# Full-row score matmuls in both attention layers; in layer 1 the softmax statistics go between partitions by DMA, and ScalarE scales the probabilities

## The chip, the cores and the metric

The kernel runs on one core of a Trainium2 chip. The metric is the device time of one execution in microseconds: the median of several runs. The engines of a core work side by side, each through its own instructions in order: TensorE (PE in the profile; PEld is its weight load), VectorE (DVE), ScalarE (ACT), GpSimd (POOL) and SyncE (SP), which issues most DMAs.

## The reference

The reference is an encoder of two layers over 512 tokens of 1024 features with 16 heads of 64 features, all in float32. Each layer adds a token mixer and then a SwiGLU channel mixer to its input, each between two RMS norms:

```python
x = x + rms_norm(mixer(rms_norm(x, g1)), g2)
x = x + rms_norm(swiglu(rms_norm(x, g3), w_gate, w_up, w_down), g4)
```

Layer 0's mixer is neighbourhood attention: a grid of 8 rows by 64 columns, each query sees all 8 rows and 16 columns around it, with a learned bias. Layer 1's mixer is a mixture of three dilated windows, (window, dilation) = (128, 1), (512, 4) and (2048, 16). Each group has its own queries, keys and values, a distance penalty per head, and a softmax over its window; the three outputs are merged with weights proportional to the softmax denominators:

```python
outs.append(o); lses.append(lse)          # one attention output and one log-sum-exp per group
alpha = jax.nn.softmax(jnp.stack(lses, axis=0), axis=0)
o = jnp.einsum('gbsh,gbshd->bshd', alpha, jnp.stack(outs, axis=0))
```

## The kernel before

**Precision.** A float32 operand is split into a high part h (rounded by a ScalarE copy, L89) and a low part l (VectorE subtracts, L90). A projection takes three matmuls for one product: h x h, h x l, l x h (`mm3`, L101 to L103).

**Projections.** The products run as units of a seven-multiplication scheme (class `Seven`): a unit loads two weight blocks of 512 KB (`load2`, L85, into a ring of two buffers), adds pieces of them on GpSimd (L168 to L174), splits four operands (`h_a`, `l_a` to `h_c`, `l_c` and a small one), and runs 84 matmuls of 256 columns into one PSUM bank. `run` interleaves a unit's last steps with the next unit's first ones.

**Attention.** Heads go in pairs; eight pairs per layer. After a pair's queries and keys are there, `split_q` lays each head's queries into 128 partitions: the high part in the head's own 64 and the low part in the other 64. `split_k` does the keys: both halves of `k` hold the head's high part, and `kl` holds the low part in 64 rows only (L429, L430). A score block then takes two matmuls into one PSUM bank (`score3` and `window_softmax` in layer 0, L435, L436, L447, L448; `scores_a` in layer 1, L953, L954): one over 128 rows with the high part of the keys, and one over the head's 64 rows with the low part.

**Layer 1's loop.** A pair has three units, one per group. `scores_a` makes the local group's scores; `scores_b` the two dilated groups' (L967), from queries and keys in token order by residue, with plain float32 matmuls of 64 rows. A chunk of scores covers one head and two blocks of 128 queries. For each block, `softmax_pair` adds the bias and takes the minimum of the negated scores in one VectorE operation (L936), and ScalarE makes the exponentials with their sum (L937). GpSimd writes the biases from a table of distances into `bt` (L941). The probabilities lie in a ring of eight buffers, `p_`, of which one pair takes all eight; the score banks, tag `s`, are two.

The local group's rows are in another order than the dilated ones: partition 32r + n of block b against partition 32b + n of block r. To merge them, `weights` swaps the local statistics (16 columns: minimum and sum, two heads, four blocks) over 32-partition pieces by 16 VectorE copies (`swapped`, L911), forms the common minimum and the two factors by small VectorE operations and one exponential, and swaps the local factors back by 16 more copies. `finish` then scales the 16 probability blocks of the pair on GpSimd (L1009), transposes them on TensorE (L1023), copies them out of PSUM (L1024) and multiplies with the values (L1031, L1037). `keep` splits the output and stores it for the output projection (`yo`).

**Order.** Python code emits the program; a planner then orders each engine's instructions by a simulated time line with priorities in the order of emission. `between` hands up to four waiting score chunks to the next unit's run, and `done` calls `finish` when all chunks of a pair are through (`left`, eight at first). Each engine's queue, SP's too, is then executed in that order.

```python
cs, js = between()
run(unit_of(i), nxt, nxt, cs)
...
done(js)
if g == 0:
    add(scores_a, j)
if g == 2:
    add(scores_b, j)
```

Of the kernel before, what the change touches and what calls it, by code (L numbers as in the profile page):

```python
# [12 lines left out]
F32 = mybir.dt.float32  # L13
# [4 lines left out]
P = 128  # L18
# [20 lines left out]
def encoder_kernel(ctx: ExitStack, tc: tile.TileContext, a: dict, out: bass.AP):  # L39
# [383 lines left out]
    def split_k(k, kl, p):  # L423
        k = k.rearrange("p (h t) -> p h t", h=2)
        act.activation(k[0:64, 0], p[0:64], AF.Copy)
        act.activation(k[64:128, 1], p[64:128], AF.Copy)
        dve.tensor_copy(k[64:128, 0], p[0:64])
        dve.tensor_copy(k[0:64, 1], p[64:128])
        dve.tensor_sub(kl[0:64], p[0:64], k[0:64, 0].bitcast(F32))  # L429
        dve.tensor_sub(kl[64:128], p[64:128], k[64:128, 1].bitcast(F32))  # L430
        return k, kl

    def score3(o, q, kd, kl, hd, qs, ks, start=True):
        r = slice(64 * hd, 64 * hd + 64)
        i = pe.matmul(o, q[(ALL, hd) + qs], kd[(ALL, hd) + ks], start=start, stop=False, skip_group_check=True)  # L435
        pe.matmul(o, q[(r, hd) + qs], kl[(r,) + ks], start=False, stop=True, skip_group_check=True)  # L436
        return i
# [4 lines left out]
    def window_softmax(q, kd, kl, hd, bt, pr, mn, sm, name):  # L442

        sb = [bank("s", f"s{name}_{i}") for i in range(2)]
        kw = kd[:, hd].rearrange("p (b t) -> p b t", b=4)[:, 0:4:3, :]
        kwl = kl[64 * hd:64 * hd + 64].rearrange("p (b t) -> p b t", b=4)[:, 0:4:3, :]
        i0 = pe.matmul(sb[0][:, 0:256], q[:, hd, 0:P], kw, start=True, stop=False, skip_group_check=True)  # L447
        pe.matmul(sb[0][:, 0:256], q[64 * hd:64 * hd + 64, hd, 0:P], kwl, start=False, stop=True,  # L448
                  skip_group_check=True)
# [374 lines left out]
    q_, k_, kl_ = ring(rxc, 0, 1152, 2), ring(rxc, 2304, D, 2), ring(rxc, 4352, 512, 2)  # L824
# [50 lines left out]
    q_, k_, kl_, ost_ = rxc[:, 0:D], rxc[:, D:2 * D], ring(rxc, 2 * D, 512, 2), ring(rxc, 3 * D, D, 1)  # L875
    w22_ = w22_ring(rxc[:, 4 * D:5 * D])
    b6 = bt.rearrange("p (k c) -> p k c", c=P)
    nc.gpsimd.dma_start(dist, a["dist"])
# [28 lines left out]
    def swapped(out_, in_):  # L907

        for i in range(4):
            for k in range(4):  # L910
                dve.tensor_copy(out_[32 * k:32 * k + 32, :, i], in_[32 * i:32 * i + 32, :, k])  # L911

    def weights(sa, sb, few):


        ta, d, w, mn, ga = (few[:, i:i + n] for i, n in ((32, 16), (48, 16), (64, 16), (80, 8), (88, 8)))
        swapped(ta.rearrange("p (s k) -> p s k", k=4), sa.rearrange("p (s k) -> p s k", k=4))
        dve.tensor_tensor(mn, ta[:, 0:8], sb[:, 0:8], op=ALU.min)
        dve.tensor_sub(d[:, 0:8], mn, ta[:, 0:8])
        dve.tensor_sub(d[:, 8:16], mn, sb[:, 0:8])  # L920
        act.activation(d, d, AF.Exp)
        dve.tensor_mul(w[:, 0:8], d[:, 0:8], ta[:, 8:16])
        dve.tensor_mul(w[:, 8:16], d[:, 8:16], sb[:, 8:16])
# [3 lines left out]
        dve.tensor_mul(w[:, 8:16], d[:, 8:16], mn)  # L927
        swapped(ga.rearrange("p (s k) -> p s k", k=4), w[:, 0:8].rearrange("p (s k) -> p s k", k=4))
        return ga, w[:, 8:16]

    def softmax_pair(pr, s, bts, st, c):

        for i in range(2):
            f = slice(256 * i, 256 * i + 256)
            o, v = (m[:, f].rearrange("p (k c) -> p k c", k=2) for m in (pr, s))
            dve.tensor_tensor_reduce(o, v, bts[i], -1.0, BIG, ALU.add, ALU.min, st[:, c + i:c + i + 1])  # L936
            act.activation(pr[:, f], pr[:, f], AF.Exp, bias=st[:, c + i:c + i + 1], scale=-1.0,  # L937
                           accum_out=st[:, 8 + c + i:9 + c + i])

    def bias(j, hd, c):  # L940
        pool.tensor_scalar(bt[:, c], dist[:, c], SLOPES[2 * j + hd], 1.0, op0=ALU.mult, op1=ALU.mult)  # L941

    def scores_a(j, hd, b2):
        rw = slice(64 * hd, 64 * hd + 64)
# [3 lines left out]
        for b in (2 * b2, 2 * b2 + 1):  # L948

            k2, l2 = ((v.rearrange("p (i t) -> p i t", i=4)[:, 0:4:3] if b == 0 else  # L950
                       v[:, P * b - P:P * b + P]) for v in (kd[:, hd], kl[rw]))
            dst = s[:, b % 2 * 256:b % 2 * 256 + 256]
            i = pe.matmul(dst, q[:, hd, block(b)], k2, start=b % 2 == 0, stop=False, skip_group_check=True)  # L953
            pe.matmul(dst, q[rw, hd, block(b)], l2, start=False, stop=True, skip_group_check=True)  # L954
            i0 = i if b % 2 == 0 else after(i, i0)
        softmax_pair(pr, s, ((b6[:, 1:3], b6[:, 0:2]), (b6[:, 0:2], b6[:, 0:4:3]))[b2], stats[j][0], 4 * hd + 2 * b2)
        parts[0, j, hd, b2] = pr

    def scores_b(j, hd, c2):
        rw = slice(64 * hd, 64 * hd + 64)  # L960
        if c2 == 0:
            bias(j, hd, slice(4 * P, 6 * P))
        s, pr = bank("s", f"sb_{j}_{hd}_{c2}"), next(p_)
        for c in (2 * c2, 2 * c2 + 1):
            for g in range(2):
                f0, (qf, kf) = c % 2 * 256 + g * P, qk[3 * j + 1 + g]
                pe.matmul(s[:, f0:f0 + P], qf[rw, block(c)], kf[rw, block(c)], start=True, stop=True)  # L967
        softmax_pair(pr, s, (b6[:, 4:6], b6[:, 4:6]), stats[j][1], 4 * hd + 2 * c2)
        parts[1, j, hd, c2] = pr

    def chunks(f, j):
        return [partial(f, j, hd, c) for hd in range(2) for c in range(2)]
# [29 lines left out]
    def finish(j):  # L1002
        ga, gb = weights(*stats[j])
        pts = []
        for hd in range(2):
            for a_b, w in enumerate((ga, gb)):
                for b in range(4):
                    v = parts[a_b, j, hd, b // 2][:, b % 2 * 256:b % 2 * 256 + 256]
                    pool.tensor_scalar(v, v, w[:, 4 * hd + b:4 * hd + b + 1], 1.0, op0=ALU.mult, op1=ALU.mult)  # L1009
# [61 lines left out]
    for n, i in enumerate(order):  # L1071
        j, g = divmod(i, 3)
        if n % 3 == 0:
            few, left[j] = next(few_), 8
            stats[j] = few[:, 0:16], few[:, 16:32], few
# [3 lines left out]
        if g == 0:  # L1079
            q = q_.rearrange("p (h t) -> p h t", h=2)  # L1080
            split_q(q, qs)
            kd, kl = split_k(k_, next(kl_), ks)
# [108 lines left out]
```

## Time and profile before

| | us |
|---|---|
| median of 3 runs (lowest, highest) | 1648.68 (1645.87, 1654.98) |
| profiled execution | 1645.9 |
| its span | 1644.1 |
| TensorE busy | 1536.3 (93%) |
| VectorE busy | 1263.6 (77%) |
| ScalarE busy | 850.2 (52%) |
| GpSimd busy | 685.7 (42%) |
| layer 0's attention loop, about | 65 to 250 |
| layer 1's attention loop, about | 830 to 1246 |

In the profile's rows, `L954` is line 954 of the kernel, the names are out<-in tiles without their numbers, and `128*128 128x256` is a matmul's rows * columns of weights and the partitions x elements of the moving operand. In the timeline a row has start, duration, engine and operation, and in brackets the idle time before it and what ended it. Matmuls overlap, and their ends are modelled: the distance from one start to the next says what one costs.

### The profile page before, as it was taken

The numbers are of one execution on the slowest core, as the hardware profiler recorded it, in microseconds if no ns is written. First come the engines' busy times: TensorE is split into PE (matmuls) and PEld (weight loads), VectorE is DVE, ScalarE is ACT, GpSimd is POOL, SyncE is SP. The second block draws the span as 40 slices with busy tenths as digits, with TensorE's granted clock in tenths as the row PEclk, the third lists the DMA queues.
The fourth block names the chain that finished last, engine by engine and source line by source line (L and its number), as shares of the span: only waits on it lengthen the run. The fifth ranks groups of instructions, "written<-read, shape, count | busy, mean of one in ns | idle before, by whom it ended". The sixth has DMA issues, their size and how long they took to land.

```text
span 1644.1 us, 28158 instructions
## 1 busy us (share of the span) xinstructions
PE 1536.3 (93%) x10788; PEld 1387.7 (84%) x10788; DVE 1263.6 (77%) x2140; ACT 850.2 (52%) x1659; POOL 685.7 (42%) x622
## 2 busy tenths in 40 slices
PE   7999999799999898879999999999998799999896
PEld 7977767799999686879988887888876799999684
DVE  5478864889998877677688788697865699998866
ACT  5356653455555555434465456455553455555554
POOL 3345432733330122465556655565613633330221
PEclk9999999899999999999999999999999899999999
DMA  4322353322322996545321231221545233323994
GB/s 167 118 66 97 122 202 128 141 78 106 120 83 71 251 239 177 175 133 163 116 84 53 78 116 65 104 77 65 195 140 169 88 103 104 103 78 97 251 243 115
DMA packets 66248, 208.80 MB, mean 127 GB/s; under 512 B 7040, under 2 KB 17280, under 8 KB 66112
## 3 DMA queue, kind: packets, MB, share of 16 engines
q1 hardware_dynamic: 53936, 164.91, 29.4%
q0 software_dynamic: 12032, 41.82, 10.6%
q8 instruction: 85, 1.39, 0.4%
q14 instruction: 51, 0.42, 0.1%
q10 hardware_dynamic: 144, 0.26, 0.0%
HBM read 184.94 MB, written 22.02 MB: 126 GB/s over the span
## 4 chain that ended last, share of the span: by engine, by line
PE 65%; DVE 14%; DMA 9%; issue 6%; POOL 3%; ACT 3%; SPq 0%; POOLq 0%; DVEq 0%; ACTq 0%
PE gu L101 9%; PE gu L102 9%; PE gu L103 9%; PE pp_d L101 3%; PE pp_d L103 3%; PE pp_d L102 3%; DMA raw<-wd 3%; DVE ap L911 2%; DMA wd<-wd 2%; PE t L1023 2%; PE yo L101 1%; PE sb L967 1%; PE yo L103 1%; PE yo L102 1%; PE pp_n L101 1%
## 5 line engine op out<-in xcount | busy, mean ns | idle before, releaser
L103 PE MATMUL gu<-rxc,l_a 128*128 128x256 f32 x352 | 102.2, 291 | 2.9 <-DVE l_a L90 2.9
L101 PE MATMUL gu<-rxc,h_a 128*128 128x256 f32 x352 | 102.8, 294 | 0.0
L102 PE MATMUL gu<-rxc,h_a 128*128 128x256 f32 x352 | 102.7, 292 | 0.0
L101 PE MATMUL gu<-rxa,h_c 128*128 128x256 f32 x352 | 100.2, 285 | 0.7 <-DVE fg L558 0.4
L101 PE MATMUL gu<-rxa,h_b 128*128 128x256 f32 x352 | 99.7, 284 | 0.2 <-ACT rxa L324 0.2
L102 PE MATMUL gu<-rxa,h_b 128*128 128x256 f32 x352 | 99.8, 284 | 0.0
L103 PE MATMUL gu<-rxa,l_c 128*128 128x256 f32 x352 | 99.6, 283 | 0.0
L102 PE MATMUL gu<-rxa,h_c 128*128 128x256 f32 x352 | 99.6, 283 | 0.0
L103 PE MATMUL gu<-rxa,l_b 128*128 128x256 f32 x352 | 99.5, 283 | 0.0
L937 ACT ACTIVATE ap<-ap 128x256 f32<-128x256 f32 x128 | 64.0, 502 | 57.0 <-DVE ap L936 56.3
L600 POOL DMA_DIRECT2D wd<-wd x36 | 34.3, 999 | 140.8 <-DVE l_d1p L90 50.3
L168 POOL TENSOR_TENSOR fg<-fg 128x512 f32<-128x512 f32 x24 | 39.8, 1657 | 121.0 <-DVE l_a L90 119.8
L168 POOL TENSOR_TENSOR r_gu<-r_gu 128x512 f32<-128x512 f32 x20 | 35.5, 1773 | 116.3 <-DVE l_a L90 116.3
L168 POOL TENSOR_TENSOR r_d<-r_d 128x512 f32<-128x512 f32 x24 | 38.0, 1584 | 97.7 <-DVE l_ad L90 97.7
L89 ACT ACTIVATE rxc<-hid 128x512 fp32r<-128x512 f32 (+1 forms) x84 | 49.2, 590 | 53.2 <-PE yd_s L102 32.8
L1009 POOL TENSOR_SCALAR ap<-ap 128x256 f32<-128x256 f32 x128 | 69.2, 560 | 15.4 <-DVE ap L927 15.2
L103 PEld LDWEIGHTS gu<-rxc,l_a 128*128 128x128 f32 x352 | 70.2, 199 | 3.1 <-DVE l_a L90 3.1
L101 PEld LDWEIGHTS gu<-rxc,h_a 128*128 128x128 f32 x352 | 70.3, 200 | 0.5 <-ACT rxc L324 0.5
L102 PEld LDWEIGHTS gu<-rxc,h_a 128*128 128x128 f32 x352 | 70.4, 200 | 0.0
L101 PEld LDWEIGHTS gu<-rxa,h_c 128*128 128x128 f32 x352 | 67.5, 192 | 1.7 <-DVE fg L558 1.5
L101 PEld LDWEIGHTS gu<-rxa,h_b 128*128 128x128 f32 x352 | 67.6, 193 | 0.5 <-ACT rxa L324 0.5
L102 PEld LDWEIGHTS gu<-rxa,h_c 128*128 128x128 f32 x352 | 67.5, 192 | 0.2
(590 smaller groups left out, 6366.7 us busy)
## 6 DMA issues: line engine op xcount, KB each, us to landing
r_d<-dil_qk SPq DMA_DIRECT2D x48, 512.0 KB, 4.5
r_d<-wd SPq DMA_DIRECT2D x30, 512.0 KB, 4.5
wd<-wd POOLq DMA_DIRECT2D x30, 512.0 KB, 9.6
fg<-wg SPq DMA_DIRECT2D x24, 512.0 KB, 3.7
fg<-wu SPq DMA_DIRECT2D x24, 512.0 KB, 4.6
r_gu<-wg SPq DMA_DIRECT2D x20, 512.0 KB, 3.7
r_gu<-wu SPq DMA_DIRECT2D x20, 512.0 KB, 4.6
r_n<-na_qk SPq DMA_DIRECT2D x16, 512.0 KB, 4.4
```

The source lines that it names most:

```text
L89: act.activation(h, src, AF.Copy)
L101: i = pe.matmul(o, s[0], m[0], start=start, stop=False, skip_group_check=True)
L102: pe.matmul(o, s[0], m[1], start=False, stop=False, skip_group_check=True)
L103: pe.matmul(o, s[1], m[0], start=False, stop=stop, skip_group_check=True)
L168: e[0].tensor_add(q[0], q[0], q[2])
L600: nc.gpsimd.dma_start(v, src, accum_op=ALU.add)
L911: dve.tensor_copy(out_[32 * k:32 * k + 32, :, i], in_[32 * i:32 * i + 32, :, k])
L937: act.activation(pr[:, f], pr[:, f], AF.Exp, bias=st[:, c + i:c + i + 1], scale=-1.0, accum_out=st[:, 8 + c + i:9 + c + i])
L967: pe.matmul(s[:, f0:f0 + P], qf[rw, block(c)], kf[rw, block(c)], start=True, stop=True)
L1009: pool.tensor_scalar(v, v, w[:, 4 * hd + b:4 * hd + b + 1], 1.0, op0=ALU.mult, op1=ALU.mult)
L1023: pe.transpose(t[:, block(i)], part(a_b, *blocks[4 * n + i]), ident)
```

## The change

Scores: `kl` becomes as wide as `k`, one half of the columns per head, with zeros in the 64 rows that are not the head's own. The matmul with the low part then runs over all 128 rows. Layer 0 has two such buffers (one of them a new tile), zeroed once; layer 1 has one, zeroed before the first pair.

Strided scores of layer 1: a chunk now makes both heads' scores for two query blocks, the matmuls of the two heads alternating, into two banks; a pair has two such chunks in place of four, so `left` starts at 6. Both heads' biases are written first, the second head's where the local bias lies.

Statistics: the two swaps of `weights` are now one DMA to a small DRAM tile and four DMAs back each, on SP's queue; the columns are in another order (block, then minimum and sum, then head), so that each piece of a row is contiguous. `finish` scales the probabilities by ScalarE activations.

```diff
     def split_k(k, kl, p):
...
-        dve.tensor_sub(kl[0:64], p[0:64], k[0:64, 0].bitcast(F32))
-        dve.tensor_sub(kl[64:128], p[64:128], k[64:128, 1].bitcast(F32))
+        kl = kl.rearrange("p (h t) -> p h t", h=2)
+        dve.tensor_sub(kl[0:64, 0], p[0:64], k[0:64, 0].bitcast(F32))
+        dve.tensor_sub(kl[64:128, 1], p[64:128], k[64:128, 1].bitcast(F32))
+    def zero_rows(kl):
+        pool.memset(kl[64:128, :512].bitcast(F32), 0.0)
+        pool.memset(kl[0:64, 512:].bitcast(F32), 0.0)
+        return kl
     def score3(o, q, kd, kl, hd, qs, ks, start=True):
-        r = slice(64 * hd, 64 * hd + 64)
         i = pe.matmul(o, q[(ALL, hd) + qs], kd[(ALL, hd) + ks], start=start, stop=False, skip_group_check=True)
-        pe.matmul(o, q[(r, hd) + qs], kl[(r,) + ks], start=False, stop=True, skip_group_check=True)
+        pe.matmul(o, q[(ALL, hd) + qs], kl[(ALL, hd) + ks], start=False, stop=True, skip_group_check=True)
...
-    def swapped(out_, in_):
-        for i in range(4):
-            for k in range(4):
-                dve.tensor_copy(out_[32 * k:32 * k + 32, :, i], in_[32 * i:32 * i + 32, :, k])
+    sw = [dpool.tile([P, 16], F32, name=f"sw{i}") for i in range(4)]
+    def swapped(out_, in_, d, n):
+        nc.sync.dma_start(d[:, :4 * n], in_)
+        for k in range(4):
+            nc.sync.dma_start(out_[32 * k:32 * k + 32].rearrange("p (i s) -> p i s", s=n),
+                              d[:, n * k:n * k + n].rearrange("(i p) s -> p i s", i=4))
...
-        swapped(ta.rearrange("p (s k) -> p s k", k=4), sa.rearrange("p (s k) -> p s k", k=4))
+        swapped(ta, sa, sw[j % 2], 4)
...
-        swapped(ga.rearrange("p (s k) -> p s k", k=4), w[:, 0:8].rearrange("p (s k) -> p s k", k=4))
+        swapped(ga, w[:, 0:8], sw[2 + j % 2], 2)
...
     def scores_a(j, hd, b2):
...
-            pe.matmul(dst, q[rw, hd, block(b)], l2, start=False, stop=True, skip_group_check=True)
+            pe.matmul(dst, q[:, hd, block(b)], l2, start=False, stop=True, skip_group_check=True)
...
-    def scores_b(j, hd, c2):
+    def scores_b(j, c2):
         if c2 == 0:
-            bias(j, hd, slice(4 * P, 6 * P))
-        s, pr = bank("s", f"sb_{j}_{hd}_{c2}"), next(p_)
+            bias(j, 0, slice(4 * P, 6 * P))
+            bias(j, 1, slice(4 * P, 6 * P), bt[:, 0:2 * P])
+        ss = [bank("s", f"sb_{j}_{hd}_{c2}") for hd in range(2)]
         for c in (2 * c2, 2 * c2 + 1):
             for g in range(2):
                 f0, (qf, kf) = c % 2 * 256 + g * P, qk[3 * j + 1 + g]
-                pe.matmul(s[:, f0:f0 + P], qf[rw, block(c)], kf[rw, block(c)], start=True, stop=True)
+                for hd in range(2):
+                    rw = slice(64 * hd, 64 * hd + 64)
+                    pe.matmul(ss[hd][:, f0:f0 + P], qf[rw, block(c)], kf[rw, block(c)], start=True, stop=True)
...
     def finish(j):
...
-                    pool.tensor_scalar(v, v, w[:, 4 * hd + b:4 * hd + b + 1], 1.0, op0=ALU.mult, op1=ALU.mult)
+                    act.activation(v, v, AF.Copy, scale=w[:, 2 * b + hd:2 * b + hd + 1])
...
-            few, left[j] = next(few_), 8
+            few, left[j] = next(few_), 6
```

More of the change, by code (lines that the diff above doesn't have):

```diff
@@ L444, in window_softmax @@
         sb = [bank("s", f"s{name}_{i}") for i in range(2)]
-        kw = kd[:, hd].rearrange("p (b t) -> p b t", b=4)[:, 0:4:3, :]
-        kwl = kl[64 * hd:64 * hd + 64].rearrange("p (b t) -> p b t", b=4)[:, 0:4:3, :]
+        kw, kwl = (v[:, hd].rearrange("p (b t) -> p b t", b=4)[:, 0:4:3, :] for v in (kd, kl))
         i0 = pe.matmul(sb[0][:, 0:256], q[:, hd, 0:P], kw, start=True, stop=False, skip_group_check=True)
-        pe.matmul(sb[0][:, 0:256], q[64 * hd:64 * hd + 64, hd, 0:P], kwl, start=False, stop=True,
-                  skip_group_check=True)
+        pe.matmul(sb[0][:, 0:256], q[:, hd, 0:P], kwl, start=False, stop=True, skip_group_check=True)
         src = [sb[0][:, 256:512], sb[1][:, 0:256], sb[1][:, 256:512]]
@@ L823, in encoder_kernel @@
     qs_, ks_, p5_ = ring(ap, 7296, 512, 2), ring(ap, 8320, 512, 2), ring(ap, 9344, 256, 2)
-    q_, k_, kl_ = ring(rxc, 0, 1152, 2), ring(rxc, 2304, D, 2), ring(rxc, 4352, 512, 2)
+    akl = inner.enter_context(arena("akl", D, "right", F32R))
+    q_, k_, kl_ = ring(rxc, 0, 1152, 2), ring(rxc, 2304, D, 2), cycle([zero_rows(v) for v in (akl, rxc[:, 4352:])])
     vq = [v_quarter(apv[:, qd * D:(qd + 1) * D], a["na_v"][qd], f"n{qd}",
@@ L874, in encoder_kernel @@
     qs, ks, p5_ = ap[:, c0 + 1728:c0 + 2240], ap[:, c0 + 2240:c0 + 2752], ring(ap, c0 + 2752, 256, 2)
-    q_, k_, kl_, ost_ = rxc[:, 0:D], rxc[:, D:2 * D], ring(rxc, 2 * D, 512, 2), ring(rxc, 3 * D, D, 1)
+    q_, k_, kl_, ost_ = rxc[:, 0:D], rxc[:, D:2 * D], rxc[:, 2 * D:3 * D], ring(rxc, 3 * D, D, 1)
     w22_ = w22_ring(rxc[:, 4 * D:5 * D])
     b6 = bt.rearrange("p (k c) -> p k c", c=P)
+    b2h = b6[:, 4:6], b6[:, 0:2]
     nc.gpsimd.dma_start(dist, a["dist"])
@@ L927, in weights, with softmax_pair @@
         dve.tensor_mul(w[:, 8:16], d[:, 8:16], mn)
-        swapped(ga.rearrange("p (s k) -> p s k", k=4), w[:, 0:8].rearrange("p (s k) -> p s k", k=4))
+        swapped(ga, w[:, 0:8], sw[2 + j % 2], 2)
         return ga, w[:, 8:16]
-    def softmax_pair(pr, s, bts, st, c):
+    def softmax_pair(pr, s, bts, st, hd, b2):
         for i in range(2):
@@ L935, in softmax_pair, with bias @@
             o, v = (m[:, f].rearrange("p (k c) -> p k c", k=2) for m in (pr, s))
[L936 to L941, printed above, removed]
+            c = 4 * (2 * b2 + i) + hd
+            dve.tensor_tensor_reduce(o, v, bts[i], -1.0, BIG, ALU.add, ALU.min, st[:, c:c + 1])
+            act.activation(pr[:, f], pr[:, f], AF.Exp, bias=st[:, c:c + 1], scale=-1.0, accum_out=st[:, c + 2:c + 3])
+    def bias(j, hd, c, o=None):
+        o = bt[:, c] if o is None else o
+        pool.tensor_scalar(o, dist[:, c], SLOPES[2 * j + hd], 1.0, op0=ALU.mult, op1=ALU.mult)
     def scores_a(j, hd, b2):
-        rw = slice(64 * hd, 64 * hd + 64)
         if b2 == 0:
@@ L966, in scores_b @@
                 f0, (qf, kf) = c % 2 * 256 + g * P, qk[3 * j + 1 + g]
-                pe.matmul(s[:, f0:f0 + P], qf[rw, block(c)], kf[rw, block(c)], start=True, stop=True)
-        softmax_pair(pr, s, (b6[:, 4:6], b6[:, 4:6]), stats[j][1], 4 * hd + 2 * c2)
-        parts[1, j, hd, c2] = pr
+                for hd in range(2):
+                    rw = slice(64 * hd, 64 * hd + 64)
+                    pe.matmul(ss[hd][:, f0:f0 + P], qf[rw, block(c)], kf[rw, block(c)], start=True, stop=True)
+        for hd in range(2):
+            pr = next(p_)
+            softmax_pair(pr, ss[hd], (b2h[hd], b2h[hd]), stats[j][1], hd, c2)
+            parts[1, j, hd, c2] = pr
     def chunks(f, j):
+        if f is scores_b:
+            return [partial(f, j, c) for c in range(2)]
         return [partial(f, j, hd, c) for hd in range(2) for c in range(2)]
@@ L1002, in finish @@
     def finish(j):
-        ga, gb = weights(*stats[j])
+        ga, gb = weights(*stats[j], j)
         pts = []
@@ L1081, in encoder_kernel @@
             split_q(q, qs)
-            kd, kl = split_k(k_, next(kl_), ks)
+            if j == 0:
+                zero_rows(kl_)
+            kd, kl = split_k(k_, kl_, ks)
         done(js)
```

21 lines of the change are left out of this document (12 added, 9 removed).

## The prediction, made before the result was known

> **What bounds the kernel now.** I read the stage table first: it gives each engine's busy time in a stretch, then the granted clock and the DMA share. The first row is layer 0's attention loop, the second layer 1's.
>
> ```profile
> 65.00:222.00 157.00, 150.41 (x973) 123.37 (x973) 121.86 (x274) 95.42 (x219) 76.59 (x95) 0.98 0.32 108
> 845.00:1250.00 405.00, 390.04 (x2919) 342.39 (x2918) 314.21 (x825) 210.39 (x535) 214.94 (x252) 0.99 0.29 98
> ```
>
> TensorE is idle for 157.00 - 150.41 = 6.6 us of the first and 405.00 - 390.04 = 15.0 us of the second; VectorE is busy 78% in both, ScalarE 61% and 52%, GpSimd 49% and 53%. TensorE is what both loops wait for. But busy is not productive, so I read the timeline of TensorE next, by the distance from one start to the next. Layer 1's local scores (L953 has 128 rows, L954 64), then layer 0's:
>
> ```profile
> 1214.70 0.28 PE L953 MATMUL sa<-rxc 128*128 128x256 f32 x1
> 1214.91 0.38 PE L954 MATMUL sa<-rxc 64*128 64x256 f32 x1
> 1215.22 0.38 PE L953 MATMUL sa<-rxc 128*128 128x256 f32 x1
> 1215.53 0.38 PE L954 MATMUL sa<-rxc 64*128 64x256 f32 x1
> 1215.84 0.50 PE L103 MATMUL yo<-rxb,rxa 128*128 128x512 f32 x1
> ```
>
> ```profile
> 162.78 0.38 PE L436 MATMUL s<-rxc 64*128 64x256 f32 x1
> 163.09 0.39 PE L435 MATMUL s<-rxc 128*128 128x256 f32 x1
> ```
>
> and a projection, where all have 128 rows, up to the longest stall of layer 1's loop:
>
> ```profile
> 1023.29 0.28 PE L102 MATMUL pp_d<-rxb,rxc 128*128 128x256 f32 x1
> 1023.41 0.28 PE L103 MATMUL pp_d<-rxb,rxc 128*128 128x256 f32 x1
> 1029.22 0.58 PE L103 MATMUL pp_d<-rxa,l_ad 128*128 128x256 f32 x1 [5.53 <-DVE l_ad L90]
> ```
>
> With equal rows a 256-column matmul starts 0.12 us after the one before. Where 128 and 64 rows alternate, the four take 0.21, 0.31, 0.31 and 0.31 us, 0.285 in the mean. The stall at 1023.41 is the other thing to see. VectorE's timeline says what l_ad waited behind:
>
> ```profile
> 1021.56 6.35 DVE L911 COPY ap<-ap 32x2 f32<-32x2 f32 x16
> 1027.94 1.23 DVE L90 TENSOR_TENSOR l_ad<-r_d,h_ad 128x1024 fp32r<-128x1024 f32 x1
> ```
>
> Sixteen statistics copies held the split that TensorE needed next.
>
> **Part 1, full-row scores.** No matmul is added or removed: the low-part ones get 128 rows, half of them zeros. The counts, from the groups of layer 1 and the view of layer 0's tile s:
>
> ```profile
> L954 PE MATMUL sa<-rxc 64*128 64x256 f32 x64 | 24.4, 381 | 0.0
> L953 PE MATMUL sa<-rxc 128*128 128x256 f32 x64 | 22.6, 353 | 0.0
> ```
>
> ```profile
> L435 PE MATMUL s<-rxc x48: 279/385/388, 99.9 to 248.3; 128*128 128x256 f32 x48
> L436 PE MATMUL s<-rxc x48: 378/382/382, 100.2 to 248.7; 64*128 64x256 f32 x48
> L447 PE MATMUL s<-rxc x16: 276/279/385, 99.3 to 246.6; 128*128 128x256 f32 x16
> L448 PE MATMUL s<-rxc x16: 379/381/383, 99.5 to 246.8; 64*128 64x256 f32 x16
> ```
>
> 128 matmuls in each layer, each from 0.285 to 0.12 us: 128 x 0.165 = 21.1 us of TensorE per layer. The Trainium skill speaks against it: TensorEngine Tiling (Array Packing), Theoretical Speedup, gives up to 2x for packing contractions of 64 rows or fewer, so by that page filling them up with zeros gives a saving away. The rows have a half-row matmul at 0.31 us and a full one at 0.12, and the measurement decides.
>
> In layer 0 nothing else changes but four half memsets on GpSimd at the start. What TensorE gives up is not all gained: its time falls to 150.41 - 21.1 = 129.3 us while VectorE keeps 121.86 us of work, in a chain with it (score, reduction, exponential, transposition). Bounds: -21 (all arrives) to -5 (157 falls to 152, VectorE's queue decides). I take two thirds, **-14 us**, since TensorE remains the longer.
>
> **Part 2, the strided scores, both heads alternating (L967).** Same count, 256. Today sixteen take 952.13 - 950.15 = 1.98 us:
>
> ```profile
> 950.15 2.05 PE L967 MATMUL sb<-ap 64*128 64x128 f32 x16
> 952.13 0.39 PE L102 MATMUL pp_d<-rxa,h_ad 128*128 128x256 f32 x1
> ```
>
> which is 0.124 each. Alternating row halves cost at least half of that if two run side by side (-0.062 x 256 = -15.9 us), and the same if they don't. I take a quarter, -4 us, nearer to the row, since all 64-row matmuls of the trace run one after another. The Trainium skill is more hopeful: TensorEngine Tiling (Array Packing), Key Properties, says that different tiles can load and multiply in parallel; by it the -15.9 us would be an estimate of the whole. No run so far shows it.
>
> **Part 3, copies to DMAs, scaling to ScalarE.**
>
> ```profile
> L1009 POOL TENSOR_SCALAR ap<-ap 128x256 f32<-128x256 f32 x128 | 69.2, 560 | 15.4 <-DVE ap L927 15.2
> L937 ACT ACTIVATE ap<-ap 128x256 f32<-128x256 f32 x128 | 64.0, 502 | 57.0 <-DVE ap L936 56.3
> L911 DVE COPY ap<-ap 32x4 f32<-32x4 f32 (+1 forms) x256 | 54.8, 214 | 4.5 <-ACT ap L937 0.6
> ```
>
> VectorE loses 54.8 us (6.9 per pair of heads), GpSimd 69.2. ScalarE gets 128 scalings; none is in the trace, the nearest row is the exponential of the same form, 502 ns: 64 us, 8.0 per pair, so it goes from 210 to about 275 busy, still under TensorE. They come sixteen in a row ahead of ScalarE's weight splits, where the copies stood ahead of VectorE's; cover taken for cover given.
>
> Two moves cost nothing. The low part of the keys has one buffer in layer 1 instead of two, but the queries and the high part have one already, so the same matmuls are waited for. And the second head's strided bias is written where the local bias lies, so the next local bias waits for its reductions; GpSimd waits for these today, with little behind it:
>
> ```profile
> POOL ap L941 <- DVE ap L936: 51.9, 17, 17.0
> ```
>
> Without that cover it would be one bias, 0.7 us per pair.
>
> The exchange is one store and four loads, twice per pair, 80 DMAs, issued by SP. Landing times and an issue:
>
> ```profile
> vd<-ap SPq DMA_DIRECT2D x20, 256.0 KB, 2.1
> ...
> ep<-spill SPq DMA_DIRECT2D x8, 64.0 KB, 6.5
> ```
>
> ```profile
> 1246.01 0.42 SPq L1103 DMA_DIRECT2D ep<-spill  x1
> ```
>
> One exchange: issue 0.42, store 2.1, four issues 1.7, last load 2.1, together 6.3 us when the queue is free, or 0.42 + 6.5 + 1.7 + 6.5 = 15.1 when crowded. With 3.5 us for the small sums on VectorE between the two exchanges and about 2 for the first four scalings, the way from the last exponential to the first transposition is X = 12.6 + 5.5 = 18 us, at most 36. I take 18: the second stage row has DMA busy at 0.29 only. Today's X and the period of a pair of heads, from the last exponentials of pairs 1, 2 and 7 and pair 2's first transposition:
>
> ```profile
> 913.79 0.50 ACT L937 ACTIVATE ap<-ap 128x256 f32<-128x256 f32 x1
> ...
> 967.34 0.49 ACT L937 ACTIVATE ap<-ap 128x256 f32<-128x256 f32 x1
> ...
> 1225.54 0.49 ACT L937 ACTIVATE ap<-ap 128x256 f32<-128x256 f32 x1
> ```
>
> ```profile
> 982.70 0.27 PE L1023 MATMUL t<-ident,ap 128*128 128x128 f32 x1
> ```
>
> The period is (1226.03 - 914.29) / 6 = 52.0 us and X = 982.70 - 967.83 = 14.9, so 37.1 us lie elsewhere in the cycle (transpositions, values, the next strided and local scores). The cycle closes because the eight probability buffers are all one pair's: the next pair's scores wait for this pair's transpositions, and in the new order the first chunk wants a second head's buffer, which is freed last.
>
> If TensorE alone sets the period, it is 52.0, less its idle 15.0 / 8 = 1.9, less (21.1 + 4) / 8 = 3.1: 47.0 us. If the cycle is strict, it is 37.1 - 3.1 + 18 = 52.0: nothing gained. Much of the 37.1 is waiting behind projection matmuls, so neither holds; I take 50.0. Over seven periods that is **-14 us**, bounds -35 to 0. It holds part 2 and the removed stalls.
>
> SP waits in order, up to 21 us for a weight buffer:
>
> ```profile
> SPq L85 <- DVE l_cd L90: 143.5, 10, 21.0
> ```
>
> A load behind an exchange is late by its wait for the statistics; these long waits are the cover, as a load has most of a unit to arrive. An exchange behind such a wait would be the worse case, the third rival.
>
> The last pair has no next pair to hide behind. Its first transposition:
>
> ```profile
> 1236.16 1.03 PE L1023 MATMUL t<-ident,ap 128*128 128x128 f32 x8
> ```
>
> 10.1 us after 1226.03, filled with output-projection matmuls to the end. With X = 18 TensorE lacks work for 8 us, less what the planner saves up for it: **+6 us** (0 to 16). The memsets of layer 1 add at most **+1**.
>
> **Sum.** -14 - 14 + 6 + 1 = -21 us. The profiled execution took 1645.9 us (span 1644.1); it becomes 1624.9. The median of the runs lies 2.8 us higher, 1648.7, so I predict 1628 for the changed kernel's median.
>
> **Rivals.** *The whole saving arrives.* For it: TensorE idles only 4% in either loop. Against: VectorE has 121.86 us to do in layer 0. Layer 1 -35, layer 0 -20, tail +5: -50, 1599 us.
>
> *ScalarE becomes the late engine.* Sixteen scalings, 8.0 us, stand ahead of the splits of the next unit, as the sixteen copies did at 1021.56. For it: that stall was 5.5 us behind 6.35. Against: it happened once in eight pairs. If half of it recurs in each, 8 x 2.8 = 22 us eat the 21: about 1649, no change.
>
> *The exchange sets the period: slower.* Place: SP's queue, where a store waits for its landing before four loads go, and 512 KB weight loads lie in between. With two of the four landings at 4.1 instead of 2.1 X is 22, the strict cycle 56.0 us, so 7 x 4.0 = +28, layer 0 -14, tail +10, memsets +1: +25, 1674 us. It makes the kernel slower as soon as the cycle is strict and 8X - 151 exceeds 8, that is above X = 20. For it: the 6.5 us row, and the longest SP waits. Against: 37.1 has slack, as TensorE was never idle in it. The Trainium skill speaks for this rival: DMA: Bandwidth & Descriptors, Rules for kernel authors, wants small transfers joined and calls those under 64 KB mostly overhead.
>
> **Chances.** Forecast 0.45, whole saving 0.25, ScalarE late 0.15, exchange 0.15. Half a per cent, 8 us, is about what a measurement of this kernel tells from none. Faster is 0.45 + 0.25 = 0.70, same 0.15, slower 0.15. The range runs from 1594 (just under the whole saving) to 1664, most of the way to the slow case; the forecast's own is 1610 to 1645.
>
> **What would show it.** Full rows: starts 0.12 us apart in both score groups, no 64-row form left there. Layer 0's loop: about 143 us instead of 157. The exchange: X near 18, and SP landings near 2.1 for the small DMAs. The cycle: last exponentials 50 us apart, 47 if TensorE alone sets it, 52 or more if strict. ScalarE: a wait of TensorE for an h or l split right behind sixteen scalings. The tail: a TensorE gap of some 6 us before the last transpositions and a lower granted clock behind it. I am wrong if small DMAs land at 4 us or more in the loop, or if layer 0 doesn't get faster while its starts are 0.12 apart.

## The result and the profile after

The changed kernel takes **1608.05 us** (median of 4 runs, 1605.10 to 1608.84), the kernel before 1648.72. The ratio is 0.9745, with a 95% interval of 0.9715 to 0.9775: about 41 us faster. In a second measurement it was 0.9741 (0.9719 to 0.9762); below I use 0.9743 for it, and turn ratios into times with 1649 us. Forecast were 1628 us and a gain of 21. So the direction was right, and the gain was about twice the forecast.

Where the 41 us come from is read from a few marks in each trace. The view by tile gives for each group the first and the last start. The first fence is the kernel before (transpositions of the output stage, local scores, transpositions of probabilities), the second the changed kernel:

```profile
L322 PE MATMUL tr_o<-ident,ep x112: 270/273/478, 283.6 to 1306.6; 128*128 128x128 f32 x112
L953 PE MATMUL sa<-rxc x64: 276/385/388, 832.1 to 1223.8; 128*128 128x256 f32 x64
L1023 PE MATMUL t<-ident,ap x256: 270/272/421, 882.2 to 1242.5; 128*128 128x128 f32 x128
```

```profile
L322 PE MATMUL tr_o<-ident,ep x112: 270/273/476, 264.3 to 1266.9; 128*128 128x128 f32 x112
L969 PE MATMUL sa<-rxc x64: 277/283/387, 813.5 to 1178.8; 128*128 128x256 f32 x64
L1046 PE MATMUL t<-ident,ap x256: 270/273/476, 855.7 to 1204.0; 128*128 128x128 f32 x128
```

| mark | before | after | gain so far |
|---|---|---|---|
| layer 0's attention done (first tr_o) | 283.6 | 264.3 | 19.3 |
| layer 1's loop begins (first sa) | 832.1 | 813.5 | 18.6 |
| last local scores (last sa) | 1223.8 | 1178.8 | 45.0 |
| last transposition (last t) | 1242.5 | 1204.0 | 38.5 |
| end of the span | 1644.1 | 1603.3 | 40.8 |

Layer 0 gives 19 us, layer 1's loop 26, and the way from the last scores to the last transposition takes 6.5 back. I call the stretch from the first sa to the last t layer 1's loop: 410.4 us before, 390.5 after.

**Full rows.** The timeline of TensorE shows local scores of the changed kernel at the same distance as a projection:

```profile
1030.59 0.28 PE L969 MATMUL sa<-rxc 128*128 128x256 f32 x1
1030.71 0.28 PE L970 MATMUL sa<-rxc 128*128 128x256 f32 x1
1030.83 0.28 PE L969 MATMUL sa<-rxc 128*128 128x256 f32 x1
```

From start to start the 128 of them take 16.7 us in all, before 38.0. The 128 of layer 0 take 19.1 us, before 37.3, so 18 less.

**Alternating heads.** Sixteen strided scores, from their start to the next matmul's:

```profile
922.27 1.49 PE L986 MATMUL sb<-ap 64*128 64x128 f32 x16
923.69 0.38 PE L101 MATMUL pp_d<-rxb,rxc 128*128 128x256 f32 x1
```

That is 1.42 us, where it was 1.98. In 73 of the 220 steps inside such groups the next matmul, of the other head, starts within 10 ns, and the pair together takes the 0.11 us that one took alone. The steps inside groups add up to 20.7 us instead of 28.2; with the steps out of them the strided scores fall from 37.4 to 29.5.

**The exchange.** Its DMAs by group (KB of each, median us from issue to landing), then an exchange in SP's timeline:

```profile
ap<-sw SPq DMA_DIRECT2D x32, 2.0 KB, 1.7
ap<-sw SPq DMA_DIRECT2D x32, 1.0 KB, 1.7
sw<-ap SPq DMA_DIRECT2D x8, 8.0 KB, 1.4
sw<-ap SPq DMA_DIRECT2D x8, 4.0 KB, 1.4
```

```profile
983.96 0.33 SPq L919 DMA_DIRECT2D sw<-ap  x1
985.37 1.75 SPq L921 DMA_DIRECT2D ap<-sw  x4
```

From the store's issue to the last load's landing this one took 4.5 us (983.96 to 988.5), which is also the median of the 16. Two exchanges, at 1084.45 and 1133.81, took 7.1 and 9.3 us, as their loads landed only after 4.3 to 6.1 us. Now the last exponentials of pairs 1 and 7, and the last pair's first transposition:

```profile
885.12 0.50 ACT L954 ACTIVATE ap<-ap 128x256 f32<-128x256 f32 x1
...
1180.84 0.49 ACT L954 ACTIVATE ap<-ap 128x256 f32<-128x256 f32 x1
```

```profile
1194.31 2.10 PE L1046 MATMUL t<-ident,ap 128*128 128x128 f32 x8 [2.67 <-ACT ap L1032]
```

The period is (1181.33 - 885.62) / 6 = 49.3 us, before 52.0. X, the way from a pair's last exponential to its first transposition, is 12.2, 12.6, 17.9, 19.5, 17.9, 20.2, 17.3 and 13.0 us for the eight pairs. The last of them ends in an idle TensorE, and in the table by stage the granted clock (third from the end, ahead of DMA share and GB/s) of the tail is lower than in the loop:

```profile
813.00:1190.00 377.00, 358.65 (x2890) 327.65 (x2889) 264.12 (x601) 258.20 (x665) 156.81 (x127) 0.99 0.33 106
1190.00:1204.00 14.00, 10.48 (x50) 6.88 (x48) 2.07 (x3) 8.06 (x19) 0.00 (x0) 0.76 0.03 1
```

Last, what TensorE waits for in layer 1's loop (total us, times, longest). Before, then after; rows under 1 us are left out:

```profile
PE pp_d L103 <- DVE l_ad L90: 5.5, 1, 5.5
PE pp_d L101 <- DVE ap L406: 5.3, 6, 1.5
PE pp_d L101 <- DVE pp_d L158: 1.2, 1, 1.2
PE pp_d L101 <- DVE ap L409: 1.2, 1, 1.2
```

```profile
PE sb L986 <- ACT ap L412: 5.5, 3, 3.0
PE pp_d L101 <- DVE ap L406: 5.2, 3, 3.3
PE t L1046 <- ACT ap L1032: 2.7, 1, 2.7
PE yo L101 <- ACT h_wo L89: 2.0, 1, 2.0
PE t L1046 <- ACT ap L1047: 1.9, 1, 1.9
PE pp_d L101 <- ACT h_ad L89: 1.2, 3, 0.4
PE pp_d L101 <- DVE ap L409: 1.1, 2, 0.7
```

The stall behind the copies (l_ad) is gone, and ScalarE's rows are new.

### The profile page after: what moved, and what is told of

Same layout as the page of the kernel before. It is cut to its first block, busy times and chain, and to the rows that moved or that the text cites. A ratio compares the mean times of both kernels' runs of the same rounds, so it can differ in the third digit from the quotient of the medians.

```text
span 1603.3 us, 28068 instructions
## 1 busy us (share of the span) xinstructions
PE 1486.7 (93%) x10788; PEld 1366.7 (85%) x10788; DVE 1205.0 (75%) x1884; ACT 897.6 (56%) x1787; POOL 628.1 (39%) x500
## 4 chain that ended last, share of the span: by engine, by line
PE 61%; DVE 12%; DMA 11%; issue 6%; ACT 5%; POOL 4%; SPq 1%; POOLq 0%; DVEq 0%; ACTq 0%
PE gu L101 9%; PE gu L102 9%; PE gu L103 9%; PE pp_d L101 4%; PE pp_d L102 3%; PE pp_d L103 3%; DMA raw<-wd 3%; DMA wd<-wd 2%; PE t L1046 2%; PE sb L986 1%; ACT ap L1032 1%; PE vd L102 1%; PE vd L101 1%; PE vd L103 1%; PE yd_pp L101 1%
## 5 line engine op out<-in xcount | busy, mean ns | idle before, releaser
L103 PEld LDWEIGHTS gu<-rxa,l_b 128*128 128x128 f32 x352 | 67.6, 192 | 0.0
```

The lines of the kernel that those rows point to most:

```text
L103: pe.matmul(o, s[1], m[0], start=False, stop=stop, skip_group_check=True)
```

## The experiments

The kernels are the changed kernel with one thing undone or altered, unless it says otherwise. A cost is the difference of its ratio from 0.9743, times 1649 us; an interval of a ratio is some 3 to 5 us wide to each side. Differences of a few us are therefore read with care, and the length of layer 1's loop in the profile is given beside them.

### Full rows undone, in one layer at a time

Layer 0 (the same in its first block of scores), and in another kernel layer 1:

```diff
 def score3(...):
-    pe.matmul(o, q[(ALL, hd) + qs], kl[(ALL, hd) + ks], ...)
+    r = slice(64 * hd, 64 * hd + 64)
+    pe.matmul(o, q[(r, hd) + qs], kl[(r, hd) + ks], ...)
```

```diff
 def scores_a(j, hd, b2):
-            pe.matmul(dst, q[:, hd, block(b)], l2, ...)
+            rw = slice(64 * hd, 64 * hd + 64)
+            pe.matmul(dst, q[rw, hd, block(b)], l2[rw], ...)
```

> The changed kernel, but layer 0's low-part scores run over the head's 64 rows again; layer 1 and the statistics as changed. Theory A (TensorE sets layer 0's pace, so its saving arrives nearly whole): 18 to 21 us above the changed kernel, about 1627, a ratio to the kernel before of 0.986 to 0.989; all of it in layer 0's loop. Theory B (as predicted: VectorE's chain eats a third): about +14, 1622. Theory C (the 19 us are mostly another order by the planner): under +10.

> The changed kernel, but layer 1's low-part local scores run over 64 rows again; layer 0 and the statistics as changed. Theory A (layer 1's loop goes at TensorE's pace, the statistics are hidden): 18 to 23 us above the changed kernel, about 1628. Theory B (a strict cycle through the statistics, or VectorE's freed time, made layer 1 faster, and TensorE's saving came through only in part): +5 to +12, 1613 to 1620.

Layer 0: 1625.81 us, ratio 0.9849 (0.9819 to 0.9880), a cost of 17 us, just under theory A's range. Layer 1: 1623.88 us, 0.9840 (0.9811 to 0.9869), a cost of 16, between the two ranges expected; its loop takes 402.7 us, 12 more than the changed kernel's. So in layer 0 nearly all of the 18 us that its score matmuls lost arrive, and VectorE's queue, which I had feared, does not decide. In layer 1, where they lost 21.3, a part is lost to other waits.

### The exchange, the scaling and the alternation undone

VectorE copies in place of the DMAs; scaling on GpSimd; both; and the strided scores one head at a time:

```diff
 def swapped(out_, in_, d, n):
-    nc.sync.dma_start(d[:, :4 * n], in_)
-    for k in range(4):
-        nc.sync.dma_start(out_[32 * k:32 * k + 32]..., d[:, n * k:n * k + n]...)
+    for i in range(4):
+        for k in range(4):
+            dve.tensor_copy(out_[32 * k:32 * k + 32, n * i:n * i + n], in_[32 * i:32 * i + 32, n * k:n * k + n])
```

```diff
-    act.activation(v, v, AF.Copy, scale=w[:, 2 * b + hd:2 * b + hd + 1])
+    pool.tensor_scalar(v, v, w[:, 2 * b + hd:2 * b + hd + 1], 1.0, op0=ALU.mult, op1=ALU.mult)
```

```diff
-def scores_b(j, c2):
+def scores_b(j, hd, c2):
...
-                for hd in range(2):
-                    rw = slice(64 * hd, 64 * hd + 64)
-                    pe.matmul(ss[hd][:, f0:f0 + P], qf[rw, block(c)], kf[rw, block(c)], start=True, stop=True)
+                pe.matmul(s[:, f0:f0 + P], qf[rw, block(c)], kf[rw, block(c)], start=True, stop=True)
```

> The changed kernel, but the statistics are swapped by VectorE copies again (32 per pair, no DMA); scaling stays on ScalarE. Theory A (TensorE sets the pace, the copies cost little where they are hidden, and the last pair's shorter way gains about 5 us): between -4 and +4 us against the changed kernel. Theory B (the removed copies are what the prediction missed in layer 1's loop, 12 us, as they stood ahead of VectorE's weight splits): +7 to +12.

> The changed kernel, but GpSimd scales the probabilities again; the exchange stays on DMAs. Theory A (off TensorE's path either way): within 3 us of the changed kernel. Theory B (GpSimd's sixteen scalings in a row held the weight additions, so that moving them was part of the gain): +5 to +12. Theory C (ScalarE late now): -5 or more.

> The changed kernel with the whole of part 3 undone: VectorE copies and GpSimd scaling, so only full rows and the alternating heads are left. Theory A (each of the two moves was worth what it cost alone: copies about +7, scaling about +13): +15 to +22 us against the changed kernel. Theory B (they take the place of one another: only both together make a pair's way to its transpositions short): +8 to +13.

> The changed kernel, but the strided scores go one head at a time again, in four chunks per pair. Theory A (as predicted, alternating heads saves a little of TensorE's switching): +3 to +8 us against the changed kernel. Theory B (it saves nothing, and freeing the banks one by one is better for the planner): -5 to 0.

| undone | us | ratio (95%) | cost, us |
|---|---|---|---|
| exchange (copies) | 1615.69 | 0.9786 (0.9757 to 0.9814) | 7 |
| scaling (GpSimd) | 1622.95 | 0.9841 (0.9812 to 0.9870) | 16 |
| both | 1630.01 | 0.9872 (0.9849 to 0.9894) | 21 |
| alternation | 1622.04 | 0.9822 (0.9800 to 0.9845) | 13 |

The exchange's 7 us are within what was expected, but in the profile the loop is only 1 us longer (391.5). Two effects hide in that. Up to the last exponential the loop takes 375.3 us with the copies and 367.8 in the changed kernel, so the DMAs gain 7.5 us there; from the last exponential to the last transposition it takes 16.2 us with the copies and 22.7 in the changed kernel, so the DMAs lose 6.5 where no next pair covers them.

The scaling and the alternation cost more than either theory had, by the medians; in the profiles the loop is 398.8 us with GpSimd scaling, 8 more than the changed kernel's, and 401.2 without the alternation, 11 more, so half of the scaling's 16 us lies outside the loop that the edit touches and isn't explained. Both moves undone cost 21 us, as theory A had it. The sum does not close: layer 1's three parts cost 16 + 21 + 13 = 50 us when undone one by one, while the loop has gained only 20. The cost of the scaling has its row in the waits of TensorE in that kernel's loop:

```profile
PE t L1046 <- POOL ap L1032: 14.3, 9, 4.2
```

With GpSimd scaling, nine times a transposition waits for a scaled block; with ScalarE this row is 2.7 us, once.

### One part alone, on the kernel before

As the costs did not add up, each part of layer 1 was also tried without the others. The first keeps the full rows of both layers and undoes the rest; the other two have half rows in both layers.

> The kernel before with the full-row scores alone (both layers): strided scores one head at a time, VectorE copies and GpSimd scaling as before. Undoing the full rows in the changed kernel cost 17 us (layer 0) and 15.5 us (layer 1). Theory additive (the parts take work from TensorE independently of one another): 1650 - 32 = 1618. Theory complement (TensorE's freed time in layer 1 is eaten by the stalls which the copies and the scaling of GpSimd cause, so that the parts gain only together; undoing the three parts of layer 1 one at a time cost 15.5 + 13.4 + 21 = 50 us where their sum is 25): layer 0 arrives whole and layer 1 by a quarter, 1650 - 17 - 5 = 1628.

> The kernel before with the exchange over DRAM and ScalarE's scaling alone: half-row scores in both layers, strided scores one head at a time. No TensorE work is taken away. Undoing this part in the changed kernel cost 21 us. Theory additive: 1650 - 21 = 1629. Theory complement: only the stalls behind the copies go (15 us of idle TensorE in the loop, less the tail's 6): 0 to -8, 1642 to 1650. The prediction's cycle argument by itself (X from 14.9 to 18, nothing taken from TensorE): 7 x 3 + 6 slower, 1677 if the cycle were strict.

> The kernel before with the strided scores of both heads alternating alone (chunks of both heads, statistics in the new order of columns); half-row local scores, VectorE copies and GpSimd scaling as before. In the changed kernel two 64-row matmuls of different row halves start 4 to 10 ns apart and 0.108 us pass until the next two, so that the steps inside the groups of strided scores add up to 20.7 us instead of 28.2. Theory additive: undoing it cost 13.4 us, so 1650 - 13 = 1637. Theory TensorE time alone: 1650 - 7.5 = 1642. Theory complement: the 7.5 us are eaten by stalls behind the copies and the scalings, 1646 to 1652.

Full rows alone: 1621.67 us, ratio 0.9830 (0.9811 to 0.9849), between its two theories and nearer to the additive one. Exchange and scaling alone: 1651.39 us, 1.0017 (1.0002 to 1.0033): no gain, so the additive theory is out, and so is the strict cycle's 1677. **Alternation alone: 1665.19 us, 1.0103 (1.0071 to 1.0135)**, 17 us slower than before. All theories missed that one, though the strided scores' steps fall in it to 28.8 us, as they should. With these, the length of layer 1's loop is known for all eight combinations (first sa to last t, one profile each; the changed kernel's two profiles differ by 1.1 us):

| us | neither | alternation | exchange and ScalarE | both |
|---|---|---|---|---|
| half rows | 410.4 | 425.2 | 416.2 | 402.7 |
| full rows | 402.3 | 407.1 | 401.2 | 390.5 |

Full rows help everywhere, by 8 to 18 us. Alternation and part 3 (the exchange with ScalarE's scaling) each cost time or bring nothing without the other (+14.8, +4.8; +5.8, -1.1), and together they are worth 8 to 12 us. Which half of part 3 the alternation needs is seen from the runs above, all with full rows and alternation: 407.1 us with copies and GpSimd scaling, 398.8 with the DMAs alone, 391.5 with ScalarE's scaling alone, 390.5 with both. ScalarE's scaling by itself does nearly all of it.

Where the alternation alone loses its time is seen at VectorE. First its timeline in that kernel, then TensorE's next start:

```profile
1141.73 7.14 DVE L923 COPY ap<-ap 32x2 f32<-32x2 f32 x16
1148.90 0.61 DVE L409 TENSOR_TENSOR ap<-ap,pp_d 128x256 f32<-128x256 f32 x1
```

```profile
1149.57 0.58 PE L101 MATMUL pp_d<-rxa,h_cd 128*128 128x256 f32 x1 [5.24 <-DVE ap L409]
```

Sixteen copies hold the instruction that empties a projection's accumulator, and TensorE waits 5.24 us for that bank. The waits of TensorE for these two evacuations, in the loop with the alternation alone, then with alternation and full rows (copies and GpSimd scaling kept in both), and last with these two and ScalarE's scaling, the copies kept:

```profile
PE pp_d L101 <- DVE ap L406: 10.6, 6, 2.8
PE pp_d L101 <- DVE ap L409: 5.4, 2, 5.2
```

```profile
PE pp_d L101 <- DVE ap L406: 16.6, 7, 4.3
PE pp_d L101 <- DVE ap L409: 3.2, 2, 3.0
```

```profile
PE pp_d L101 <- DVE ap L406: 5.5, 3, 2.2
...
PE pp_d L101 <- DVE ap L409: 0.7, 3, 0.3
```

Before they were 5.3 and 1.2, and with full rows alone 11.3 and 1.2. With the alternation alone TensorE is idle for 27.9 us of the loop, before for 14.9; these two rows are 9.5 us of the 13. So with the copies and GpSimd's scaling both in place, TensorE time that is saved comes back as waiting for VectorE. The copies alone don't do it: in the last kernel they stand in VectorE's queue as before, and the rows are short.

### How tight the cycle is

One more small DMA in each exchange:

```diff
 def swapped(out_, in_, d, n):
-    nc.sync.dma_start(d[:, :4 * n], in_)
+    nc.sync.dma_start(d0[:, :4 * n], in_)
+    nc.sync.dma_start(d[:, :4 * n], d0[:, :4 * n])
...
```

> Changed kernel, with one more small DMA (DRAM to DRAM, 128 rows of 64 or 32 bytes) between the store and the four loads of each exchange. A store of the changed kernel landed after 1.4 us, so each exchange gets about 2 us longer and the way X from the last exponential to the first transposition about 4 us. Theory strict (the cycle through the probability buffers sets the period): 7 periods x 4 us and 4 us in the tail, +32 us against the changed kernel's 1608, about 1640. Theory slack (the scores, projections and transpositions of a pair can shift against each other, and only some pairs wait): the tail's 4 us and at most a quarter of the periods, +4 to +11, 1612 to 1619. Between the two, the share of the 28 us that arrives is the share of pairs in which the exchange ends the wait.

It took 1631.12 us, ratio 0.9882 (0.9854 to 0.9910): a cost of 23 us, much nearer to the strict theory. X rises from 16.3 to 20.5 us in the mean of the eight pairs, the period of pairs 1 to 7 from 49.3 to 51.9: some 0.6 us for each us of X, in the mean; most of it falls on pairs 5 and 6, whose X is 29.9 and 28.1. A shorter X doesn't gain in the same way: with the copies undone above X is 11.8 in the mean, and the period 50.1. TensorE waits for the scaling and for ScalarE's weight split behind it:

```profile
PE t L1048 <- ACT ap L1034: 13.6, 4, 6.6
PE pp_d L101 <- ACT h_ad L89: 6.7, 3, 5.6
```

The next two begin with the kernel that has the alternation alone. One leaves out the second head's strided bias (both heads use the first's), so that GpSimd needn't wait for its place; the other scales and transposes both heads' strided probabilities first, so that the buffers that the next pair's first chunk wants are freed first:

```diff
-            bias(j, 1, slice(4 * P, 6 * P), bt[:, 0:2 * P])
-    b2h = b6[:, 4:6], b6[:, 0:2]
+    b2h = b6[:, 4:6], b6[:, 4:6]
```

```diff
 def finish(j):
-        for hd in range(2):
-            for a_b, w in enumerate((ga, gb)):
+        for a_b, w in ((1, gb), (0, ga)):
+            for hd in range(2):
...
-            for a_b, blocks in enumerate((a8, b8)):
+        for a_b, blocks in ((1, b8), (0, a8)):
+            for hd in range(2):
```

> The kernel with the alternating strided scores alone (17 us slower than the kernel before), and in it the second head's strided bias is left out: both heads use the first head's, so this part of the computation is changed. GpSimd then no longer waits for the local scores' reductions before it can write a strided bias, nor for the strided ones before the next local bias; in the kernel with the alternation alone these waits had grown from 51.9 to 74.0 us, with the scalings and the weight additions queued behind them. Theory bias (that queue is the cause): at least 12 of the 17 us go, 1640 to 1652. Theory buffers (the first strided chunk wants a buffer of the second head, which is freed last): within 4 us of the kernel with the alternation alone, 1661 to 1668. Of the two, 8 instructions of 0.3 to 0.7 us on GpSimd less make no difference of their own.

> The kernel with the alternating strided scores alone, and in it both heads' strided probabilities are scaled and transposed ahead of both heads' local ones, so that the buffers which the next pair's first strided chunk wants come free after half of the transpositions instead of all. Theory buffers: at least 12 of the 17 us go, 1640 to 1652. Theory bias: within 4 us of the kernel with the alternation alone, 1661 to 1668. VectorE's waits for transpositions ahead of its reductions (4.8 us in 5 times with the alternation alone) should go with this order under either theory.

Without the bias: 1664.62 us, ratio 1.0085 (1.0058 to 1.0112), not told apart from 1.0103, although GpSimd's waits for the bias's place fell from 74.0 to 49.1 us. With the other order: 1647.53 us, **0.9971 (0.9947 to 0.9996)**, 22 us less by the ratios (18 by the medians, 11 in the loops of the profiles). The reductions' waits for transpositions, alternation alone and then with the order changed:

```profile
DVE ap L954 <- PE t L1048: 4.8, 5, 2.3
```

```profile
DVE ap L954 <- PE t L1049: 0.6, 1, 0.6
```

So the alternation alone loses only with the old order of freeing the buffers, as the theory of the buffers had it. That the buffers themselves are the reason is shown for these waits, which are 4 of the 22 us. The planner also places everything anew when the order changes: TensorE's two waits for evacuations fall to 7.0 and 1.7 us with the copies still there, and 99 steps of the strided scores pair where 62 did. How the rest divides was not separated, and the new order was not tried without the alternation, so it may be worth something there too.

### A faster version

VectorE copies for the last pair alone, where nothing is left that could cover the exchange; and the same with the order of the experiment above:

```diff
 def swapped(out_, in_, d, n, j):
+    if j == PAIRS - 1:
+        for i in range(4):
+            for k in range(4):
+                dve.tensor_copy(out_[32 * k:32 * k + 32, n * i:n * i + n], in_[32 * i:32 * i + 32, n * k:n * k + n])
+        return
     nc.sync.dma_start(d[:, :4 * n], in_)
```

> The changed kernel, but the last pair's two swaps are VectorE copies, the other seven pairs' stay DMAs. Theory A (the last pair's way lies open, as predicted with 6 us): -3 to -6 us against the changed kernel. Theory B (TensorE has other work to hide it): within 2 us.

> The changed kernel with VectorE copies for the last pair (1604.0 us in its own run), and in it both heads' strided probabilities are scaled and transposed ahead of both heads' local ones. With the exchange over DRAM and ScalarE's scaling the way X from the last exponential to the first transposition is unchanged, but the next pair's first chunk can start after half of the transpositions (about 5 us earlier where it waits for them). Theory strict (the cycle through the buffers still costs time in the changed kernel, as the longer exchange did): up to 7 x 2 us faster, 1590 to 1599. Theory slack: 1602 to 1607.

The first: 1603.97 us, ratio 0.9722 (0.9702 to 0.9742), as theory A had it; in its profile the loop takes 383.8 us, 6.7 less than the changed kernel's, and the way from the last exponential to the last transposition is 16.5 us instead of 22.7. The second: **1599.06 us, 0.9694 (0.9680 to 0.9709)**, loop 376.8, at the edge of the strict theory's range. It beats both kernels, by about 50 and about 8 us. The order's own share is some 5 us, with intervals that overlap a little; it agrees with a buffers' cycle that still costs time in the changed kernel, but the planner's new placement isn't told from it here either.

## Why the prediction was right or wrong

**What bounds the kernel: right.** TensorE sets both loops; full rows help in every combination.

**Part 1, the price: right.** 128 x 0.165 = 21.1 us was forecast per layer; layer 1's local scores fell by 38.0 - 16.7 = 21.3, layer 0's by 18.

**Layer 0, "I take two thirds, -14": wrong in size.** The mark at the end of its attention moved by 19.3, and undoing it costs 17. What failed is the step that gave VectorE's 121.86 us a say; TensorE's waits in layer 0's loop of the changed kernel stay short (the longest three rows), and all that the score matmuls gave up arrived:

```profile
PE ta L477 <- POOL ap L858: 2.1, 2, 1.1
PE tb L479 <- POOL ap L858: 2.0, 1, 2.0
PE pp_n L101 <- DVE pp_n L158: 1.2, 1, 1.2
```

**Part 2, "a quarter, -4": wrong in size, and its reason was wrong.** It was 7.9 us, half of the bound of 15.9. The reason, that all 64-row matmuls of the trace run one after another, holds for the strided scores, where neighbours always used the same row half, but not for the whole trace: three times in layer 0 of the kernel before, a score matmul and a transposition of 64 rows started 5 ns apart. One of them:

```profile
112.36 0.38 PE L436 MATMUL s<-rxc 64*128 64x256 f32 x1
112.37 0.27 PE L470 MATMUL ta<-ident,ap 64*128 64x64 f32 x1
```

With opposite halves the strided scores run side by side, in 73 of the 128 pairs that could form. The Trainium skill's rule (TensorEngine Tiling (Array Packing), Key Properties: different tiles can work in parallel) agrees with the 73 pairs that start within 10 ns.

**Part 3.** The exchange was forecast at 6.3 us and took about 4.5: the small DMAs land after 1.4 and 1.7 us instead of the 2.1 of a 256 KB load, and the time to landing, which is counted from the issue, already holds the issues that the sum added to it. The sign "small DMAs land at 4 us or more" did come up, in the loads of two exchanges of sixteen. X at 18 was right for the pairs in the middle of the loop (17.3 to 20.2). The period was forecast at 50.0 us and is 49.3. **The step that failed is "over seven periods that is -14".** The first period, from pair 0 to pair 1, fell from 49.8 to 42.1 us, so 7.7 at once, and the start of the loop up to pair 0's last exponential by 2.4. Seven periods gave 23.7 (7.7, and 2.7 for each of the other six), with the start 26.1. I took 2.0 from the steady part for all, chosen between the two bounds; the gain is closer to TensorE alone (-35) than to the strict cycle (0). The sum also let X grow by 3 everywhere, from pair 2's 14.9. Pairs 1 to 7 did grow, by 2.8 to 6.0 us, but pair 0's X was 17.6 before and fell to 12.2. VectorE's timeline before, behind pair 0's last exponential at 864.53:

```profile
872.30 0.15 DVE L927 TENSOR_TENSOR ap<-ap 128x8 f32<-128x8 f32 x1
...
875.17 3.75 DVE L911 COPY ap<-ap 32x2 f32<-32x2 f32 x16
```

The small sums ended 7.9 us after the exponential, with weight splits between them, and the copies another 6.5 us later. In the changed kernel the sums end 5.2 us after it, and the exchange takes 4.5. That this shorter way is why the first period fell was not tested by itself. Of the 20 us that the forecast missed, the seven periods are 10, layer 0 is 5, the start 2, and 2 lie behind the loop, where nothing was changed.

**The tail, +6: right, though not for its reason alone.** From the last exponential (1226.03, then 1181.33: 44.7 gained) to the last transposition (38.5 gained) 6.2 us are given back, and the kernel with VectorE copies for the last pair wins them back. The sum had only lack of work in it, though a lower clock stood among the signs. In that stretch TensorE is idle for 3.5 us, before for 0.6, so that is 2.9; the other 3.3 are slower work, as the granted clock there is 0.85 in the mean and was 1.00.

The memsets' +1 can't be seen: 18.9 us are gained at the start of layer 1's value projections and 18.6 at its first local scores.

**Named, but priced at nothing:** "the first chunk wants a second head's buffer, which is freed last". Its missing price is large, about 20 us where the alternation is alone and about 5 in the changed kernel, as far as the order of freeing shows it. It works against the gain, so it isn't what made the forecast too small. The bias's place, which I also took to cost nothing, cost nothing that could be told.

**The rivals.** *ScalarE late* did occur, at two places. Timelines of ScalarE, VectorE and TensorE in the changed kernel:

```profile
946.35 3.31 ACT L1032 ACTIVATE ap<-ap 128x256 f32<-128x256 f32 x8 [3.02 <-DVE ap L943]
949.56 1.04 ACT L89 ACTIVATE h_bd<-r_d 128x1024 fp32r<-128x1024 f32 x1
```

```profile
950.64 1.22 DVE L90 TENSOR_TENSOR l_bd<-r_d,h_bd 128x1024 fp32r<-128x1024 f32 x1 [3.47 <-ACT h_bd L89]
951.78 0.41 DVE L406 TENSOR_TENSOR ap<-ap,pp_d 128x256 f32<-128x256 f32 x1
```

```profile
952.25 0.38 PE L101 MATMUL pp_d<-rxb,h_cd 128*128 128x256 f32 x1 [3.33 <-DVE ap L406]
...
1100.22 1.01 PE L986 MATMUL sb<-ap 64*128 64x128 f32 x6 [3.05 <-ACT ap L412]
```

Eight scalings hold a weight's high part on ScalarE, VectorE waits for it with its low part, and behind that stands the evacuation that TensorE wants: 3.33 us. With 3.05 us at 1100.22, where a strided score waits for ScalarE's L412 behind eight scalings, these two waits come to 6.4 us, not 22; the scalings take 0.41 us each (3.31 / 8), not the 0.502 of an exponential, and seldom stand more than eight in a row. *The exchange sets the period* didn't happen, since X stayed under 20 for all pairs but one (20.2), but its premise was nearer to the truth than I allowed: 4 us more of X cost 23. *The whole saving arrives* was the likelier case for layer 0 and for the loop up to its tail.

## What to carry to other kernels

Price a change on an engine that sets the loop at its full bound first, and take off only what a named wait will take; a cautious fraction has no row behind it. Parts that use the same buffers or the same queue are not to be summed: an edit that loses 17 us alone was worth 13 beside another, and only runs of the combinations told which part needs which. Where a cycle through buffers closes, free first what the next turn asks for first, and price the end of a loop by itself, since a latency that is hidden in every turn shows in the last.

## What the runs showed of the hardware that was not expected

Two 64-row matmuls of 128 columns that use different row halves and write different banks start within 10 ns and take 0.11 us together, while 64-row and 128-row ones in turn cost 0.285 us each instead of 0.12. So padding with zeros and packing both took TensorE time away here, each where its neighbours fitted. A DMA of 1 to 8 KB through DRAM landed after 1.4 to 1.7 us in the median, and five of them in a chain of two took about 4.5, beside 3.4 us of VectorE's time in the mean for the sixteen copies that they replaced (54.8 us for 16 swaps; 6.35 in the one that stalled TensorE). The scaling of a 128x256 block took 0.41 us on ScalarE and 0.56 on GpSimd; moved back to GpSimd it cost 16 us by the medians, 8 of them in the loop.

A stall of TensorE costs more than its wait. In both kernels' layer 1 loops each stall of 2.7 us or more has a granted clock of one half for 3.4 or 6.8 us beside or behind it, one such stretch before and three in the changed kernel.
